# Low parts of the second FFN's down weights: from a subtraction on VectorE to a negated cast on ScalarE and an accumulating DMA

## The chip, the cores and the metric

The kernel runs on one core of a Trainium2 chip. A core has five engines with a queue of instructions each: TensorE (PE, matrix products), VectorE (DVE), ScalarE (ACT), GpSimd (POOL) and SyncE (SP, which issues the transfers), and 16 DMA engines between the memory and the on-chip buffer. An engine works through its queue in order and waits on semaphores. The metric is the device time of one execution in microseconds.

## The reference

Two decoder layers over 512 tokens of width 1024, each `x += gate1 * Mixer(adaLN(x))` and `x += gate2 * ConvFFN(adaLN(x))`. Layer 0 mixes by attention, layer 1 by a state-space layer and a gated delta rule. The change touches only the FFN of layer 1:

```python
def conv_ffn(h, w_up, conv_w, w_down):
    up = causal_dwconv(h @ w_up, conv_w)
    a, b = jnp.split(up, 2, axis=-1)
    return (jax.nn.silu(a) * b) @ w_down
```

`w_up` is 1024 x 5632, `w_down` 2816 x 1024, all in float32.

## The kernel before

Activations lie transposed, 128 channels on the partitions and 512 tokens in a row. Every large product is made of three: each float32 factor is split into a high part, rounded to the type fp32r, and a low part, which is the factor minus its high part; the product is high x high, high x low and low x high, added up in one bank of PSUM (`mm3`, L374 to L376). So every weight needs two tiles, `whi` and `wlo`.

A weight is got ready by `prep` (L343 to L361): SP loads it into a staging tile `st` (L356, two of them in turn), ACT casts it to `whi` (L359), and DVE writes `wlo` as `st` minus `whi` (L360). There are five tiles `whi` and five `wlo` in turn; a cast waits until PE has done with the weight that held the tile before. `weight` asks for a weight one or two places ahead of its use, in the order of `weight_order`.

The second FFN (`ffn` with l = 1) goes over 22 channel blocks j of the up projection. The first four are plain products. From j = 4 a pair of up weights is made into seven smaller products of 256 columns (`prep_pair`, L315 to L341, and `seven`, L594 to L627). `prep_pair` uses the same staging tiles for its loads of an even block (L321 and L322), and the same tiles `whi` and `wlo`; DVE adds in the staging tiles (L335 to L339) and subtracts (L328), ACT casts (L327). In `seven`, ACT copies intermediate products from PSUM (L610, tiles p1, p7 and p16), and PE goes on with the same bank after that; DVE makes `ub` and `ua` (L620 to L624). `finish` does the convolution, the SiLU (L657) and the split of the result into `gh` and `gl`.

The down projection is cut by GROUPS into four groups of 6, 6, 5 and 5 blocks, with 8 weights each: 32 down weights (`dn`, 1), 16 of 128 x 768 and 16 of 128 x 640. The weights of a group come one or two per block among the up products of the next group, a product of 18 or 15 matmuls of 512 columns each (L374 to L376 with `gh` and `gl`); those of the last group come at the end (`out_gemm`). A DVE instruction then adds the result to x (L479), and SP stores x (L1612).

The order of the instructions on each engine is set when the program is built, by a scheduler that goes by priorities and dependences. Nothing is issued to POOL in this FFN before the change.

Of the kernel before, what the change touches and what calls it, by code (L numbers as in the profile page):

```python
# [8 lines left out]
F32 = mybir.dt.float32  # L9
F32R = mybir.dt.float32r  # L10
I32 = mybir.dt.int32
AF = mybir.ActivationFunctionType
ALU = mybir.AluOpType
# [176 lines left out]
def down_after(l, j):  # L190
# [3 lines left out]
    if q == 0:  # L194
        return []
    if not SPREAD[l]:
        return [(q - 1, m) for m in range(8 if j == g[q] else 0)]
# [43 lines left out]
SPLIT_AT = (18, 18, 18, 18)  # L241
FAST = ((), tuple(range(4, 22)))
SPREAD = (False, True)
REC_K = (2, 3, 4, 5, 0, 1, 6, 7)


class Kernel:
# [95 lines left out]
    def prep(self, pool=None, stage=None):  # L343
        key = self.order[self.next]
        self.next += 1
        if key[0] == "sp":
            self.ready[key] = self.prep_pair(*key[1:])
            return
        src, n = self.source(key)
        nc = self.nc  # L350
        wp = pool or self.wp
        if stage:
            st = stage[0].tile([P, 1024], F32, name="ast", tag=stage[1], bufs=stage[2])[:, :n]
        else:
            st = wp.tile([P, 1024], F32, name="st", tag="st", bufs=1 if pool else 2)[:, :n]
        nc.sync.dma_start(st, src)  # L356
        hi = wp.tile([P, 1024], F32R, name="whi", tag="whi", bufs=1 if pool else 5)[:, :n]
        lo = wp.tile([P, 1024], F32R, name="wlo", tag="wlo", bufs=1 if pool else 5)[:, :n]
        nc.scalar.copy(hi, st)  # L359
        nc.vector.tensor_tensor(lo, st, hi.bitcast(F32), ALU.subtract)  # L360
        self.ready[key] = (hi, lo)  # L361

    def weight(self, key):
# [730 lines left out]
    def recurrent(self):  # L1094
# [450 lines left out]
        rhs = self.pairs(self.hB)  # L1545
        for n, a in zip(REC_K, SPLIT_AT):
            self.tc.cur_priority = at[a]
            self.split(Y[n], *rhs[n], half=n < 2)
        self.tc.cur_priority = end
        for n in REC_K[len(SPLIT_AT):]:  # L1550
            self.split(Y[n], *rhs[n], half=n < 2)
# [6 lines left out]
        self.keep, self.keep_pool = {}, self.open("fg1", "right")  # L1558
        self.out_gemm([("ro", m) for m in range(8)], rhs, lambda m: self.gate(1, 0, m), 1, 1, hC, REC_K, ("acc", "acc", "t", "x", "s", "s", "o", "o"))
        self.close("hB")  # L1560
# [90 lines left out]
```

## Time and profile before

| what | value |
|---|---|
| median of 3 runs | 1306.91 us (1306.52 to 1307.76) |
| the profiled execution | 1305.8 us |
| its span | 1304.0 us |
| PE busy in the span | 1280.3 us (98%) |
| DVE busy | 1011.4 us (78%) |
| ACT busy | 638.8 us (49%) |
| POOL busy | 3.6 us |
| clock of TensorE | full speed in every slice |
| DMA, mean | 139 GB/s |

The span is what the profile covers; the profiled execution took 1.8 us more than that, and its time is 1.1 us below the median. The share of an engine is a mean over stages with different limits. A matmul's end is modelled and matmuls overlap, so the distance from one start to the next tells PE's pace better than the durations. A row of the chain or the timeline that names a releaser in brackets says how long the engine was idle before that instruction and what ended the wait.

### The profile page before, as it was taken

How to read it: one execution, taken by the hardware profiler on the slowest of the kernel's cores; microseconds unless marked ns; L12 is line 12 of the kernel's file. 1: busy time of each engine (PE TensorE's matmuls, PEld its weight loads, DVE VectorE, ACT ScalarE, POOL GpSimd, SP SyncE). 2: the span in 40 equal slices, each digit the busy share in tenths (PEclk: the TensorE clock that was granted, in tenths of full speed). 3: DMA queues.
4: the chain of work that ended last, by engine and by line, in shares of the span. 5: the costliest groups of instructions: out<-in, count | busy, mean ns of one | idle time of the engine just before them, and what ended most of it. 6: DMA issues, size and time to landing. Idle time of an engine off the chain costs nothing.

```text
span 1304.0 us, 22696 instructions
## 1 busy us (share of the span) xinstructions
PE 1280.3 (98%) x8814; PEld 1085.3 (83%) x8814; DVE 1011.4 (78%) x2227; ACT 638.8 (49%) x1246; POOL 3.6 (0%) x11
## 2 busy tenths in 40 slices
PE   8989999999999999999999999999999999999998
PEld 5976776798886888888898888887898998999998
DVE  6886856579996589477578786775699988988883
ACT  4446566435441333233357545654475655555550
POOL 0000000000000000000000000000000000000000
PEclk9999999999999999999999999999999999999999
DMA  9763511425655477454343531221322322333222
GB/s 364 272 226 118 186 59 48 164 105 192 213 163 169 159 263 241 154 185 157 106 176 127 140 111 44 102 60 34 130 98 98 105 102 102 102 102 99 96 85 102
DMA packets 83131, 181.13 MB, mean 139 GB/s; under 512 B 28560, under 2 KB 36176, under 8 KB 83024
## 3 DMA queue, kind: packets, MB, share of 16 engines
q1 hardware_dynamic: 83024, 179.69, 40.8%
q8 instruction: 69, 1.13, 0.3%
q14 instruction: 38, 0.31, 0.1%
HBM read 165.55 MB, written 14.11 MB: 138 GB/s over the span
## 4 chain that ended last, share of the span: by engine, by line
PE 86%; DVE 6%; DMA 3%; ACT 2%; issue 2%; SPq 0%; DVEq 0%; ACTq 0%
PE acc L374 10%; PE acc L375 10%; PE acc L376 10%; PE s L375 5%; PE s L376 5%; PE s L374 5%; PE o L375 4%; PE o L376 4%; PE o L374 4%; PE s L606 3%; PE s L776 3%; PE o L606 3%; PE acc L606 3%; PE o L805 2%; DMA ast<-ada 1%
## 5 line engine op out<-in xcount | busy, mean ns | idle before, releaser
L359 ACT CAST whi<-st 128x1024 fp32r<-128x1024 f32 (+3 forms) x168 | 165.2, 987 | 213.5 <-PE acc L375 69.6
L360 DVE TENSOR_TENSOR wlo<-st,whi 128x1024 fp32r<-128x1024 f32 (+3 forms) x168 | 191.5, 1142 | 50.8 <-ACT whi L359 49.3
L374 PE MATMUL acc<-hh,whi 128*128 128x512 f32 (+1 forms) x392 | 141.1, 365 | 0.5 <-ACT hh L530 0.5
L375 PE MATMUL acc<-hl,whi 128*128 128x512 f32 (+1 forms) x392 | 140.9, 363 | 0.2 <-DVE hl L394 0.2
L376 PE MATMUL acc<-hh,wlo 128*128 128x512 f32 (+1 forms) x392 | 140.8, 362 | 0.0
L445 DVE CUSTOM_DVE_ANT_0 adaj<-ast,cond 128x1024 bf16<-128x1024 f32 x86 | 105.0, 1221 | 11.9 <-DMA ast<-ada 11.5
L375 PE MATMUL acc<-wlo,hh 128*128 128x256 f32 x320 | 92.9, 291 | 0.0
L374 PE MATMUL acc<-whi,hh 128*128 128x256 f32 x320 | 92.1, 288 | 0.6 <-ACT hh L530 0.6
L376 PE MATMUL acc<-whi,hl 128*128 128x256 f32 x320 | 91.3, 287 | 0.9 <-DVE hl L531 0.9
L375 PE MATMUL s<-hl,whi 128*128 128x512 f32 (+2 forms) x256 | 86.8, 339 | 0.0
L376 PE MATMUL s<-hh,wlo 128*128 128x512 f32 (+2 forms) x256 | 86.6, 338 | 0.0
L374 PE MATMUL s<-hh,whi 128*128 128x512 f32 (+2 forms) x256 | 86.4, 338 | 0.0
L375 PEld LDWEIGHTS acc<-hl,whi 128*128 128x128 f32 x392 | 73.3, 188 | 12.7 <-DVE hl L394 1.2
L374 PEld LDWEIGHTS acc<-hh,whi 128*128 128x128 f32 x392 | 73.1, 188 | 12.2 <-ACT hh L530 0.8
L376 PEld LDWEIGHTS acc<-hh,wlo 128*128 128x128 f32 x392 | 73.4, 188 | 11.2 <-issue 0.7
L327 ACT CAST whi<-st 128x1024 fp32r<-128x1024 f32 x54 | 56.4, 1049 | 32.5 <-DVE st L339 9.3
L328 DVE TENSOR_TENSOR wlo<-st,whi 128x1024 fp32r<-128x1024 f32 x54 | 65.9, 1222 | 4.4 <-ACT whi L327 4.4
L374 PE MATMUL o<-hh,whi 128*128 128x512 f32 (+1 forms) x192 | 69.0, 359 | 0.0
L375 PE MATMUL o<-hl,whi 128*128 128x512 f32 (+1 forms) x192 | 68.9, 359 | 0.0
L376 PE MATMUL o<-hh,wlo 128*128 128x512 f32 (+1 forms) x192 | 68.8, 358 | 0.0
L374 PEld LDWEIGHTS acc<-whi,hh 128*128 128x128 f32 x320 | 60.3, 188 | 4.9 <-issue 3.2
L375 PEld LDWEIGHTS acc<-wlo,hh 128*128 128x128 f32 x320 | 60.3, 188 | 3.9 <-issue 3.7
(910 smaller groups left out, 3498.7 us busy)
## 6 DMA issues: line engine op xcount, KB each, us to landing
ast<-ada SPq DMA_DIRECT2D x92, 512.0 KB
st<-up SPq DMA_DIRECT2D x88, 512.0 KB
st<-ri SPq DMA_DIRECT2D x20, 512.0 KB
st<-wq SPq DMA_DIRECT2D x17, 512.0 KB
st<-dn SPq DMA_DIRECT2D x16, 448.0 KB
st<-dn SPq DMA_DIRECT2D x16, 384.0 KB
st<-dn SPq DMA_DIRECT2D x16, 320.0 KB
st<-wo SPq DMA_DIRECT2D x8, 512.0 KB
```

What stands on the lines that cost most here:

```text
L327: nc.scalar.copy(hi, src)
L328: nc.vector.tensor_tensor(lo, src, hi.bitcast(F32), ALU.subtract)
L359: nc.scalar.copy(hi, st)
L360: nc.vector.tensor_tensor(lo, st, hi.bitcast(F32), ALU.subtract)
L374: mm(out, lh, rh, start=start, stop=False)
L375: mm(out, lh, rl, start=False, stop=False)
L376: mm(out, ll, rh, start=False, stop=stop)
L445: self.nc.vector.tensor_tensor_reduce(junk, st, self.cond, 1.0, 0.0, op0=ALU.mult, op1=ALU.add, accum_out=self.md[l][:, i:i + 1])
L606: nc.tensor.matmul(acc, x[:, s], y, start=start and k == n == 0, stop=k == 3 and n == 2, skip_group_check=not start)
L776: nc.tensor.matmul(sb, qT[pr, i * P:(i + 1) * P], kT[pr, j0 * P:(i + 1) * P], start=True, stop=True)
L805: nc.tensor.matmul(ob[64 * par:64 * par + 64, i * P:(i + 1) * P], V[:, j0 + j, vc:vc + 64], pts[:, par, j * P:(j + 1) * P], start=j == 0, ...
```

## The change

For the weights whose key begins with ("dn", 1), the low part is made in another way. ACT casts the staged weight to `whi` as before. Then ACT also writes minus `whi` into `wlo`, and POOL issues a transfer that reads the weight from memory a second time and adds it to what stands in `wlo`. DVE has no part in it. All other weights are made as before.

```diff
+DMA_LOW = (("dn", 1),)
...
         nc.scalar.copy(hi, st)
-        nc.vector.tensor_tensor(lo, st, hi.bitcast(F32), ALU.subtract)
+        if key[:2] in DMA_LOW:
+
+            nc.scalar.activation(lo, hi.bitcast(F32), AF.Copy, scale=-1.0)
+            nc.gpsimd.dma_start(lo, src, accum_op=ALU.add)
+        else:
+            nc.vector.tensor_tensor(lo, st, hi.bitcast(F32), ALU.subtract)
```

Lines behind L360 move down by six. So L374, L375 and L376 become L380, L381 and L382, L606 becomes L612 and L610 becomes L616; the new cast is L363 and the new transfer L364. L327 and L328 become L328 and L329 by one, and L359 becomes L360.

The scheduler also sets another order. First, ACT at the first down weight. Before (whi_11062 is the high part of that weight; whi_11070 belongs to the next pair of up weights):

```order
L610 COPY p7_11121<-x_11091 128x256
L359 CAST whi_11062<-st_11060 128x768
L327 CAST whi_11070<-st_11066 128x1024
L610 COPY p16_11135<-t_11090 128x256
L657 ACTIVATE ta_11046<-ta_11046 128x512
```

ACT at the same place, changed:

```order
L616 COPY p7_11122<-x_11092 128x256
L360 CAST whi_11062<-st_11060 128x768
L328 CAST whi_11071<-st_11067 128x1024
L363 ACTIVATE wlo_11063<-whi_11062 128x768
L616 COPY p16_11136<-t_11091 128x256
L663 ACTIVATE ta_11046<-ta_11046 128x512
```

The new cast stands behind the cast of the up weight and ahead of the copy p16.

Second, PE at the same weight (the product goes into the bank acc; rows of products that are alike are left out). Before, with no other product between the high and the low part:

```order
L606 MATMUL t_11090<-b30l_10367,whi_10938 128x256
L606 MATMUL t_11090<-b30h_10366,wlo_10939 128x256
L374 MATMUL acc_11203<-gh_10604,whi_11062 128x512
L375 MATMUL acc_11203<-gl_10605,whi_11062 128x512
L376 MATMUL acc_11203<-gh_10604,wlo_11063 128x512
```

PE at the same place, changed:

```order
L380 MATMUL acc_11204<-gh_10604,whi_11062 128x512
L381 MATMUL acc_11204<-gl_10605,whi_11062 128x512
L612 MATMUL s_11255<-hh0_10080,whi_11071 128x256
L612 MATMUL t_11091<-b00h_10324,whi_10938 128x256
...
L612 MATMUL t_11091<-b30h_10366,wlo_10939 128x256
L612 MATMUL s_11255<-hl0_10081,whi_11071 128x256
...
L612 MATMUL s_11255<-hh3_10086,wlo_11072 128x256
L612 MATMUL o_11257<-hh4_10088,whi_11071 128x256
L382 MATMUL acc_11204<-gh_10604,wlo_11063 128x512
```

Between the first high and the first low part now stand the 12 products into t, which stood ahead of the weight before, and 13 more into s and o.

Third, ACT at the third down weight (whi_11369 before, whi_11371 changed). Before:

```order
L610 COPY p1_11415<-t_11398 128x256
L327 CAST whi_11249<-st_11229 128x1024
L657 ACTIVATE ta_11352<-ta_11352 128x512
L610 COPY p7_11429<-x_11399 128x256
L359 CAST whi_11369<-st_11367 128x768
```

ACT at the same place, changed:

```order
L328 CAST whi_11251<-st_11231 128x1024
L360 CAST whi_11371<-st_11369 128x768
L616 COPY p1_11419<-t_11402 128x256
L663 ACTIVATE ta_11354<-ta_11354 128x512
L363 ACTIVATE wlo_11372<-whi_11371 128x768
L616 COPY p7_11433<-x_11403 128x256
```

The high cast of the down weight has moved ahead of the copy p1. Behind the first steps the order of PE differs at two more places by a few rows, and is the same from there on.

## Rows read from the trace of the kernel before

**Rows 1.** Windows: busy time of each engine, clock, DMA share, GB/s.

```profile
core 0: us, PE busy (x) PEld busy (x) DVE busy (x) ACT busy (x) POOL busy (x), PEclk, DMA share, GB/s
1026.00:1304.00 278.00, 271.97 (x1879) 251.03 (x1877) 228.07 (x334) 138.36 (x217) 0.00 (x0) 1.00 0.29 101
```

**Rows 2.** Timeline of PE: start us, us, instruction, idle before and releaser.

```profile
1085.27 0.28 PE L606 MATMUL acc<-hh,wlo 128*128 128x256 f32 x1
1087.16 0.39 PE L606 MATMUL acc<-b01h,vhi 128*128 128x256 f32 x1 [1.61 <-ACT p L610]
...
1204.14 0.28 PE L606 MATMUL acc<-hh,wlo 128*128 128x256 f32 x1
1204.97 0.38 PE L606 MATMUL x<-hh,whi 128*128 128x256 f32 x1 [0.56 <-DVE ub L622]
...
1234.47 0.28 PE L606 MATMUL s<-hh,wlo 128*128 128x256 f32 x1
1235.14 0.38 PE L606 MATMUL acc<-hh,whi 128*128 128x256 f32 x1 [0.40 <-DVE ub L622]
```

**Rows 3.** Chain that ended last, 1066 to 1237: start us, us, what.

```profile
1068.21 0.96 DVE wlo L360
...
1069.19 4.53 DMA st<-up
...
1080.31 4.20 DMA st<-dn
...
1084.54 0.84 ACT whi L359
...
1196.37 3.99 DMA st<-up
...
1226.50 1.37 PE acc L606 x12
...
1228.26 3.91 DMA st<-up
```

**Rows 4.** Groups by form, 1020 to 1304: count, busy us, mean ns, idle before.

```profile
L360 DVE TENSOR_TENSOR wlo<-st,whi 128x768 fp32r<-128x768 f32 x16 | 15.3, 954 | 1.7 <-ACT whi L359 1.7
L359 ACT CAST whi<-st 128x768 fp32r<-128x768 f32 x16 | 13.4, 838 | 10.5 <-DMA st<-dn 4.4 <-PE s L375 3.2 <-PE o L375 2.1
L360 DVE TENSOR_TENSOR wlo<-st,whi 128x640 fp32r<-128x640 f32 x16 | 13.1, 822 | 1.4 <-ACT whi L359 1.4
L359 ACT CAST whi<-st 128x640 fp32r<-128x640 f32 x16 | 11.6, 729 | 15.9 <-DMA st<-dn 6.8 <-PE acc L375 5.4 <-PE acc L606 2.3
```

**Rows 5.** Timeline of ACT at five down weights.

```profile
1024.16 0.84 ACT L359 CAST whi<-st 128x768 fp32r<-128x768 f32 x1 [0.34 <-DMA st<-dn]
1024.90 1.05 ACT L327 CAST whi<-st 128x1024 fp32r<-128x1024 f32 x1
...
1051.85 0.84 ACT L359 CAST whi<-st 128x768 fp32r<-128x768 f32 x1 [0.18 <-DMA st<-dn]
...
1066.72 0.83 ACT L359 CAST whi<-st 128x768 fp32r<-128x768 f32 x1
...
1124.41 0.84 ACT L359 CAST whi<-st 128x768 fp32r<-128x768 f32 x1
...
1284.74 0.73 ACT L359 CAST whi<-st 128x640 fp32r<-128x640 f32 x1 [4.13 <-DMA st<-dn]
```

**Rows 6.** Timeline of SP's queue, 1048 to 1050.

```profile
1048.99 0.33 SPq L356 DMA_DIRECT2D st<-dn  x1
```

**Rows 7.** Timeline of PE: first reads of three down weights' low parts.

```profile
1028.71 0.39 PE L376 MATMUL acc<-gh,wlo 128*128 128x512 f32 x1
...
1138.46 0.39 PE L376 MATMUL x<-gh,wlo 128*128 128x512 f32 x1
...
1292.10 0.28 PE L376 MATMUL acc<-gh,wlo 128*128 128x256 f32 x1
```

**Rows 8.** Waits of ACT, 1026 to 1304: us in total, times, longest.

```profile
ACT p L610 <- PE s L606: 8.4, 9, 1.8
```

## The prediction

> **What bounds the kernel now.** I read the views in this order: the busy time of the stretch that the change touches, the few places where TensorE (PE) idles there, the chain that leads to each of them, then the subtraction that goes, then how early each low part is needed.
>
> The stretch runs from 1026 us, where the first subtraction for a down weight of the second FFN stands, to the end. In its 278 us PE is busy for 271.97, VectorE (DVE) for 228.07, ScalarE (ACT) for 138.36, GpSimd (POOL) not at all, and the DMA engines have a share of 0.29 [rows 1]. A busy PE is not always PE at its pace, so I take the pace from starts: twelve products of 256 columns took 1.37 us, 0.114 each [rows 3]. PE falls out of that pace at three places behind 1026. From the start of one matmul to that of the next it took 1.89 us at 1085.27, 0.83 at 1204.14 and 0.67 at 1234.47 where 0.11 is the rule [rows 2]. That is 1.78 + 0.72 + 0.56 = 3.1 us, and it is nearly all that PE can get back: the stretch is bound by PE, and DVE is the engine that is late at these places.
>
> The chain shows why, with the largest one. The subtraction L360 of a down weight starts at 1068.21 and frees a staging tile; the load of an up weight follows (4.53 us), then a run of DVE work, then a load of a down weight (4.20 us), its cast on ACT at 1084.54, and behind that cast the copy of a product for which PE waits at 1087.16 [rows 2, 3]. The gaps at 1204.97 and 1235.14 are waits for DVE's ub [rows 2]; the chain to each holds a load of an up weight into a staging tile, issued at 1196.37 and 1228.26 [rows 3].
>
> **The change, part by part.** *Removed:* 32 subtractions on DVE, 16 of 0.954 us and 16 of 0.822 [rows 4], 28.4 us of DVE's 228. DVE is not on PE's path except at the three places, so the worth is at most their 3.1 us. I take all of it, because two things come together. DVE has some 0.9 us less to do per down weight. And the staging tile is now free when the high part's cast ends: the cast that belongs to 1068.21 ran from 1066.72 for 0.83 us [rows 5], so the tile is free at 1067.6 where the load waited until 1069.19 [rows 3]; 1.6 us earlier, almost the 1.78 of the gap behind it. Term: -3.1 us. What cover this needs: ACT must not be late in its turn.
>
> *Added on ACT:* 32 times minus the high part, ACT from fp32r tile to tile. I price them as the casts of the same tile sizes, 16 of 0.838 and 16 of 0.729 us [rows 4], 25.1 us. ACT is busy for half of the stretch [rows 1], and it mostly waits for PE when it copies products (L610): 9 waits for the s banks alone are 8.4 us [rows 8]. The new casts fall into such waits. I take 0. Queued behind a new cast on ACT are the copies of products (p), the SiLU and the next high part. Where the cover is gone it costs up to 1.7 us once: at the third down weight the order puts its high cast, which waited for a landing until 1051.85 [rows 5], ahead of the copy p1; PE has one other product of 1.4 us to do in that time. With PE already late by the next term, it is hidden.
>
> *Added on POOL and the DMA queue:* 32 accumulating transfers, 16 of 384 KB and 16 of 320 KB, 11.5 MB more than the 28 MB (101 GB/s in 278 us) that the stretch moves now. The share of 0.29 [rows 1] grows to 0.41, or to 0.53 if the old low part is counted as read too; bandwidth is not the limit. POOL has nothing else queued there [rows 1]. SP's queue keeps the 32 loads of the staging tile, so every down weight is now read twice from memory.
>
> *The path from weight to matmul.* Before: high cast, subtraction (0.95 us), matmul. Now: high cast, low cast, transfer, matmul. No transfer issued by POOL and none that accumulates is in the trace, so its time T from the end of the low cast to the release of PE is bounded. Below: a plain load of the same 384 KB, issued at 1048.99 and waited for by ACT until 1051.85, 2.9 us [rows 5, 6]. Above: twice the slowest load of that size, 4.20 us [rows 3], 8.4. A gain is excluded, since nothing gets ready sooner by it. I take twice the quick load, 5.7 us: two operands of that size come in, and the queue is lightly used, so the quick load is the nearer row.
>
> The transfer is late where PE comes soonest after the high cast. That is the first down weight: its cast starts at 1024.16, another cast of 1.05 us at 1024.90 stands behind it, and PE read the low part at 1028.71 [rows 5, 7]. In the new order the low cast stands behind that second cast, so it ends at 1024.90 + 1.05 + 0.84 = 1026.8; and PE has 13 more products of 256 columns ahead of the first low part, 13 x 0.114 = 1.5 us, so it comes at 1030.2. With T = 5.7 the tile is there at 1032.5: PE waits for 2.3 us. The bounds of T give 0 and 5.0.
>
> For later weights the same sum finds no wait. A usual one: high cast from 1124.41 for 0.84 us, low part read at 1138.46 [rows 5, 7], 13.2 us apart. The tightest late one is the last weight of all: cast from 1284.74 for 0.73 us, read at 1292.10 [rows 5, 7], 6.6 us apart; its load too goes out earlier, by about the 1.6 us above, so low cast and transfer have 8.2 us where 0.73 + 5.7 = 6.4 are needed.
>
> *By the skill's price:* the Trainium skill (DMA: Bandwidth & Descriptors, section "Anatomy of one DMA — SWDGE (gpsimd) path") fits transfers issued by GpSimd as 2.0 us plus the bytes at 436 GB/s, for 384 KB an estimate of 2.9 us. No run here shows such a transfer, and the fit is for plain ones; by it the first weight's wait is 0 and the sum -3.1, so 1303.8.
>
> *Sum.* The profiled execution took 1305.8 us (span 1304.0), 1.1 below the median of 1306.91. 1305.8 - 3.1 + 0 + 2.3 = 1305.0 in its own terms, 1306.1 in terms of the median. With T at its bounds: 1303.8 and 1308.8. So I forecast no difference that can be told: a measurement of this kernel tells about 0.2%, 2.6 us, apart.
>
> **The rivals.** *Faster.* The transfer is as quick as a plain load (T near 2.9), PE never waits for a low part, and all three gaps close: 1306.9 - 3.1 = 1303.8. For it: nothing else uses POOL, and the DMA engines are idle for 0.71 of the stretch [rows 1]. Against it: two operands instead of one, a longer hand-over (ACT, POOL, queue, PE), and there is no more than 3.1 us to have, so any wait above 0.5 us ends it.
>
> *Slower: the accumulating transfer itself is slow.* Place: PE's first low part, and then every weight that PE reads within T of its cast. It decides from a first wait of 3.1 + 2.6 = 5.7 us, thus T = 9.1 us. For T = 12: 1026.8 + 12 - 1030.2 = 8.6 us at the first weight. The last weight would be late by 12 + 0.73 - 8.2 = 4.5 us, but PE itself then comes 8.6 - 3.1 = 5.5 later, so it adds none; 1306.9 - 3.1 + 8.6 = 1312.4. Above T = 13 the usual distance of 13.2 us [rows 5, 7] doesn't cover it either, and each further us adds at many weights. For it: the operation was never seen here, and reads its destination. Against it: engines that are idle for most of the time.
>
> *Slower: DVE holds back GpSimd.* If POOL can prepare transfers only while DVE is idle, 0.18 of the time [rows 1], a microsecond of preparation becomes 1 / 0.18 = 5.5 us. T = 5.7 + 4.5 = 10.2, the first wait 6.8 and the time 1306.9 - 3.1 + 6.8 = 1310.6. The rule is in the Trainium skill (SBUF — State Buffer, section "Who interferes with whom"): GpSimd and DVE share a port pair, and an instruction of DVE in a 2-port mode shuts GpSimd out. The page also says that tensor_tensor has no such mode, and that is most of what DVE runs here; no run here shows it, as POOL is idle.
>
> *The change does nothing:* that PE is bound and both terms are small is the forecast itself.
>
> **How the numbers follow.** Forecast 0.45 (1304.3 to 1309.5, its own range, with T between 3.9 and 9.1), faster 0.24, slow transfer 0.25, DVE against GpSimd 0.06. So faster 0.24, same 0.45, slower 0.31. The range goes down to 1303.3 (the faster case, with half a us for what the pace itself regains) and up to 1315 (T near 13); above it lies the rest of the slow transfer, some 0.12, and below it some 0.05.
>
> **What would show it.** Right: PE's one new wait stands at the first read of a low part near 1030 and is 1 to 4 us long, released by a DMA; the gaps at 1085, 1204 and 1235 are gone or under 0.3 us; DVE's busy time falls by 28 us, ACT's grows by about 25; low tiles land 4 to 8 us after POOL's issue. Wrong: PE waits for a low part at many weights (then T is above 9), ACT's copies of products are late behind the new casts (then PE's waits name ACT), or the three gaps stay (then DVE was not what they hung on). It would be wrong in the other direction if PE never waits.

## The result

The changed kernel is slower: 1317.41 us, median of 5 runs (1315.17 to 1325.87), beside 1307.76 for the kernel before (1306.52 to 1309.59). The ratio is 1.0078, with a 95% interval of 1.0055 to 1.0102, so about 10 us. The prediction was 1306.1, with a range that ended at 1315.0.

| run | what is changed | ratio to the kernel before | 95% interval |
|---|---|---|---|
| the changed kernel | all 32 low parts by transfer | 1.0078 | 1.0055 to 1.0102 |
| r1_cast_behind | one order edge on ACT | 1.0073 | 1.0051 to 1.0094 |
| r2_both | that edge, first weight on DVE | 1.0067 | 1.0040 to 1.0094 |
| r3_no_transfer | ACT writes, DVE adds | 1.0003 | 0.9989 to 1.0017 |
| r4_first_on_vector | first weight on DVE | 1.0053 | 1.0032 to 1.0073 |
| r5_transfers_only | kernel before plus transfers that nobody reads | 1.0179 | 1.0157 to 1.0201 |
| r6_cast_ahead | kernel before, a cast ahead of a copy | 1.0003 | 0.9991 to 1.0016 |
| r7_loads_in_turn | other order of loads on SP | 1.0056 | 1.0035 to 1.0078 |
| r8_half_transfer | half by transfer, half by DVE | 1.0105 | 1.0088 to 1.0122 |
| r9_changed_without_transfers | the transfers left out | 0.9968 | 0.9947 to 0.9990 |
| r10_plain_transfers | plain transfers, not adding | 1.0015 | 0.9993 to 1.0038 |
| r11_every_other | every other weight, the rest on DVE | 1.0006 | 0.9985 to 1.0026 |
| r12_half_bytes | half the columns of each transfer | 1.0024 | 1.0006 to 1.0043 |
| r13_half_number | every other transfer | 1.0013 | 0.9995 to 1.0030 |
| r14_three_weights | the new way for three weights | 0.9976 | 0.9966 to 0.9986 |

Each ratio goes against runs of the kernel before that were taken with it (their medians lie between 1307.8 and 1311.0 us), so the ratios are to be compared, and not the times. They are the ratios on record; the ratio of the two medians lies up to 0.0014 from them (r10), so a difference of 0.001 between two rows tells nothing. r9, r10, r12 and r13 leave out a part of the low parts' arithmetic and serve for timing alone.

### The profile page after: what moved, and what is told of

It reads as the page before. It is cut to its first block, busy times and chain, and to the rows that moved or that the text cites. A ratio compares the mean times of both kernels' runs of the same rounds, so it can differ in the third digit from the quotient of the medians.

```text
span 1315.6 us, 22783 instructions
## 1 busy us (share of the span) xinstructions
PE 1285.0 (98%) x8814; PEld 1089.4 (83%) x8814; DVE 988.7 (75%) x2195; ACT 659.2 (50%) x1278; POOL 31.1 (2%) x43
## 5 line engine op out<-in xcount | busy, mean ns | idle before, releaser
L360 ACT CAST whi<-st 128x1024 fp32r<-128x1024 f32 (+3 forms) x168 | 165.0, 985 | 215.9 <-PE acc L381 65.6
L366 DVE TENSOR_TENSOR wlo<-st,whi 128x1024 fp32r<-128x1024 f32 (+1 forms) x136 | 162.8, 1199 | 49.0 <-ACT whi L360 47.5
L380 PE MATMUL acc<-hh,whi 128*128 128x512 f32 (+1 forms) x392 | 141.1, 365 | 1.4 <-ACT hh L536 1.3
L381 PE MATMUL acc<-hl,whi 128*128 128x512 f32 (+1 forms) x392 | 140.8, 362 | 0.2 <-DVE hl L400 0.2
L382 PE MATMUL acc<-hh,wlo 128*128 128x512 f32 (+1 forms) x392 | 140.7, 362 | 0.0
L451 DVE CUSTOM_DVE_ANT_0 adaj<-ast,cond 128x1024 bf16<-128x1024 f32 x86 | 104.7, 1218 | 11.2 <-DMA ast<-ada 10.9
L381 PE MATMUL acc<-wlo,hh 128*128 128x256 f32 x320 | 93.3, 292 | 0.0
L380 PE MATMUL acc<-whi,hh 128*128 128x256 f32 x320 | 92.4, 289 | 0.6 <-ACT hh L536 0.6
L382 PE MATMUL acc<-whi,hl 128*128 128x256 f32 x320 | 91.6, 288 | 0.9 <-DVE hl L537 0.9
L381 PE MATMUL s<-hl,whi 128*128 128x512 f32 (+2 forms) x256 | 86.7, 339 | 0.0
L380 PE MATMUL s<-hh,whi 128*128 128x512 f32 (+2 forms) x256 | 86.4, 337 | 0.0
L382 PE MATMUL s<-hh,wlo 128*128 128x512 f32 (+2 forms) x256 | 86.4, 337 | 0.0
L380 PEld LDWEIGHTS acc<-hh,whi 128*128 128x128 f32 x392 | 73.1, 188 | 13.1 <-ACT hh L536 1.6
L381 PEld LDWEIGHTS acc<-hl,whi 128*128 128x128 f32 x392 | 73.3, 188 | 12.6 <-DVE hl L400 1.2
L382 PEld LDWEIGHTS acc<-hh,wlo 128*128 128x128 f32 x392 | 73.3, 188 | 11.2 <-issue 0.7
L329 DVE TENSOR_TENSOR wlo<-st,whi 128x1024 fp32r<-128x1024 f32 x54 | 65.7, 1218 | 5.1 <-ACT whi L328 4.9
L328 ACT CAST whi<-st 128x1024 fp32r<-128x1024 f32 x54 | 56.3, 1046 | 25.6 <-PE o L612 5.6
L380 PE MATMUL o<-hh,whi 128*128 128x512 f32 (+1 forms) x192 | 69.0, 359 | 0.0
L382 PE MATMUL o<-hh,wlo 128*128 128x512 f32 (+1 forms) x192 | 69.0, 359 | 0.0
L381 PE MATMUL o<-hl,whi 128*128 128x512 f32 (+1 forms) x192 | 68.9, 359 | 0.0
L380 PEld LDWEIGHTS acc<-whi,hh 128*128 128x128 f32 x320 | 60.4, 189 | 4.9 <-issue 3.2
L381 PEld LDWEIGHTS acc<-wlo,hh 128*128 128x128 f32 x320 | 60.3, 188 | 3.9 <-issue 3.7
```

The lines of the kernel that those rows point to most:

```text
L328: nc.scalar.copy(hi, src)
L329: nc.vector.tensor_tensor(lo, src, hi.bitcast(F32), ALU.subtract)
L380: mm(out, lh, rh, start=start, stop=False)
L381: mm(out, lh, rl, start=False, stop=False)
L382: mm(out, ll, rh, start=False, stop=stop)
L451: self.nc.vector.tensor_tensor_reduce(junk, st, self.cond, 1.0, 0.0, op0=ALU.mult, op1=ALU.add, accum_out=self.md[l][:, i:i + 1])
```

## The profile after

First the stretch of [rows 1]. The row below has the same columns: the stretch, busy us and counts of PE, PEld, DVE, ACT and POOL, the granted clock, the DMA share and GB/s.

```profile
1026.00:1304.00 278.00, 269.94 (x1832) 248.99 (x1831) 204.27 (x300) 160.11 (x251) 27.80 (x32) 0.99 0.53 139
```

DVE lost 24 us of work, ACT took on 22, POOL does nothing but issue the 32 transfers, and the DMA share went from 0.29 to 0.53. Here the old gaps of [rows 2] are not to be found; PE waits elsewhere. These are the four waits above 1 us in the timeline of PE (start, us, instruction, idle before and releaser), each with the matmul before it:

```profile
1030.89 0.28 PE L612 MATMUL o<-hh,whi 128*128 128x256 f32 x1
1033.48 0.50 PE L382 MATMUL acc<-gh,wlo 128*128 128x512 f32 x1 [2.32 <-DMA wlo<-dn]
...
1104.41 0.28 PE L612 MATMUL o<-b31h,vlo 128*128 128x256 f32 x1
1106.01 0.38 PE L612 MATMUL s<-b00h,whi 128*128 128x256 f32 x1 [1.33 <-ACT p L616]
...
1137.95 0.28 PE L612 MATMUL o<-b31h,vlo 128*128 128x256 f32 x1
1140.16 0.45 PE L612 MATMUL o<-b00h,whi 128*128 128x256 f32 x1 [1.92 <-ACT p L616]
...
1173.40 0.28 PE L612 MATMUL t<-b31h,vlo 128*128 128x256 f32 x1
1176.12 0.39 PE L612 MATMUL o<-b00h,whi 128*128 128x256 f32 x1 [2.44 <-ACT p L616]
```

From start to start, less the 0.11 us that a product of 256 columns takes, they cost 2.48, 1.49, 2.10 and 2.61 us, 8.7 in all. The first is the late low part that was forecast. The other three were not: PE waits for ACT's copy `p16` (L616). Why the copy is late stands in ACT's own timeline at the first of them:

```profile
1100.84 0.35 ACT L616 COPY p<-s 128x256 f32<-128x256 f32 x1
1101.10 0.62 ACT L399 CAST gh<-tb 128x512 fp32r<-128x512 f32 x1
1101.89 0.37 ACT L616 COPY p<-o 128x256 f32<-128x256 f32 x1 [0.18 <-PE o L612]
1105.07 0.62 ACT L328 CAST vhi<-st 128x512 fp32r<-128x512 f32 x1 [2.81 <-DMA st<-up]
1105.60 0.37 ACT L616 COPY p<-s 128x256 f32<-128x256 f32 x1
```

The two copies at 1100.84 and 1101.89 are `p1` and `p7`. The third, `p16`, stands behind the cast `vhi`, and that cast belongs to the next pair: it waits 2.81 us for an up load to land, with the copy that PE needs queued behind it. In the chain of waits (start, us, what) the load is the long piece:

```profile
1098.84 0.84 ACT whi L360
...
1099.69 5.35 DMA st<-up
...
1105.07 0.03 ACT vhi L328
```

In [rows 3] loads of up weights take 3.91 to 4.53 us; here 5.35, and at the two other waits 5.80 and 6.32 (issued at 1133.39 and 1168.84).

There is a second loss behind two of the waits. The rows below are of the granted clock (the last number but two), in windows of 1 us after the wait that ends at 1033.48:

```profile
1033.00:1034.00 1.00, 0.52 (x2) 0.47 (x3) 1.00 (x2) 0.21 (x1) 0.00 (x0) 1.00 0.00 0
1034.00:1035.00 1.00, 1.00 (x5) 0.77 (x5) 1.00 (x2) 0.00 (x0) 0.00 (x0) 0.76 0.20 37
1035.00:1036.00 1.00, 1.00 (x7) 1.00 (x6) 0.17 (x1) 0.00 (x0) 0.00 (x0) 0.50 0.89 299
```

The clock is at its lower level, 1.2 GHz, from within 1034 to within 1037. The wider windows around the two falls give what it took: 0.95 over 1030 to 1035, 0.71 over 1035 to 1040 and 0.83 over 1140 to 1150, so 5 x 0.05 + 5 x 0.29 + 10 x 0.17 = 3.4 us, 1.7 for each fall. Behind the waits of 1106 and 1176 the clock stayed at 1.00.

## The experiments

### Theory and rivals

At first I held that ACT's new order did it (theory A: `vhi` ahead of `p16`), with these rivals: the transfers make the loads late (B), the first late low part and its clock (C), ACT's 25 us of casts as such (D).

**The cast behind the copy.** The edge is written at the trace of a pair: its `vhi` cast may not be issued ahead of the last `p16` traced.

```diff
-        f["22"], = halves(b[:, T:], self.fp, "v", 2)
...
+            with self.tc.issue_after(self.p16.ins):
+                f["22"], = halves(b[:, T:], self.fp, "v", 2)
...
```

> The changed kernel with one order edge more: the cast of a pair's second load (vhi) may not be issued on ScalarE ahead of the copy p16 of the pair before. In the changed kernel's profile TensorE waited 1.49, 2.10 and 2.61 us for that copy, which stood behind a vhi cast that waited 2.81, 3.37 and 3.88 us for its load, and the granted clock fell once after one of these waits (about 1.7 us). One of the three places in which the cast stands ahead of the copy is left by this edge. Theory A (ScalarE's order makes the loss): 1317.4 - 6.2 - 1.7 = 1309.5 us, up to 1312 if the place that is left still waits. Rival B (the accumulating transfers slow the loads, and TensorE then waits for the loads themselves): 1317, with the same waits under another name. Rival C (only the first late low part and its clock matter): 1317. Rival D (25 us more work on ScalarE): 1317.

Measured 1.0073: nothing won. The waits for `p16` went, and others came in their place, of 3.77, 1.68 and 1.84 us from start to start, for DVE's `ub`; the first low part was late by 3.29 us in that profile, the slowest execution of the six. DVE's timeline at the first of them shows the same queue on the other engine:

```profile
1111.88 0.69 DVE L329 TENSOR_TENSOR vlo<-st,vhi 128x512 fp32r<-128x512 f32 x1 [5.82 <-ACT vhi L328]
1112.48 0.42 DVE L632 SCALAR_TENSOR_TENSOR ub<-o,p 128x256 f32<-128x256 f32 x1
...
1114.02 0.42 DVE L634 SCALAR_TENSOR_TENSOR ub<-s,p 128x256 f32<-128x256 f32 x1
```

`vlo` of the next pair stands ahead of `ub` of this one, and waits through `vhi` for the same load. So ACT's order decides where PE feels the late load, but not whether it does. Theory A fell here in its simple form.

**The first down weight on DVE again**, alone (r4) and with the edge (r2). The edit takes out one weight, the first of the first column group, in r2 too (the expectation speaks of one in each group):

```diff
-        if key[:2] in DMA_LOW:
+        if key[:2] in DMA_LOW and key[2:] != (0, 0):
```

> The changed kernel, the low part of the first down weight alone (first row block of the first column group) made by VectorE as before; ScalarE's order is else that of the changed kernel, cast ahead of copy at most pairs. Theory A and C: the first wait (2.5 us) and the halved clock behind it (1.7 us) go, the waits for the copy p16 stay: 1317.4 - 4.2 = 1313.2 us. If the first wait were the whole of the loss: 1307. If a wait costs no clock: 1314.9.

> The same order edge, and the low part of the first down weight of each column group, first row block, is made by VectorE as before, so that no accumulating transfer stands in front of the stage's first down matmuls. Theory A with C: 1309.5 less the first wait of 2.5 us and the clock after it of 1.7 us: 1305.3 us. Rival B: about 1313 (only the first wait goes). Rival D: 1313.

Measured 1.0053 and 1.0067. The wait at 1030 is gone in both, though in r2 another low part is late by 2.02 us, at 1062. Both intervals overlap that of the changed kernel: a gain of 4.2 us would be 0.3%, and the ratios leave 0.1 to 0.25%. In r4's profile the three waits for `p16` grew, to 1.98, 2.54 and 3.23 us (6.2 us in the changed kernel, 7.75 here). The longest of them:

```profile
1172.98 0.28 PE L612 MATMUL t<-b31h,vlo 128*128 128x256 f32 x1
1176.32 0.38 PE L612 MATMUL o<-b00h,whi 128*128 128x256 f32 x1 [3.06 <-ACT p L616]
```

PE comes to the same places sooner, and the loads take longer: 5.70, 6.25 and 7.08 us in the chain, where the changed kernel has 5.35, 5.80 and 6.32. Rival C is out as the whole of the loss. What the first wait is worth alone these intervals don't tell: they hold both nothing and the 4.2 us.

**No transfer, DVE adds.**

```diff
-            nc.gpsimd.dma_start(lo, src, accum_op=ALU.add)
+            nc.vector.tensor_tensor(lo, lo.bitcast(F32), st, ALU.add)
```

> No accumulating transfer at all: ScalarE still writes minus the high part (25 us more on ScalarE), and VectorE adds the staged weight to it. ScalarE's order comes out as that of the run with both edits, with the copy p16 ahead of the casts nearly everywhere. Theory A: no loss from ScalarE's work as such, 1306 to 1309 us. Rival B (transfers): 1306 to 1309 as well, but with the loads of the up weights back at 3.9 to 4.5 us where the run with both edits shows over 5.3. Rival D (ScalarE's load): 1313 or more.

Measured 1.0003. ACT has its extra 25 us here and nothing is lost, so rival D is out. Waits of 1.87, 0.73 and 1.10 us from start to start stand near the places of the old gaps, so nothing is won there either. The order was not that of the run with both edits, as I had written: SP's order came out as in the kernel before, since DVE reads the staging tile again. The run doesn't tell A from B therefore.

**The order without transfers**, in the kernel before:

```diff
...
-        p16 = keep(Z, "p16")
+        with self.tc.issue_after(self.vcast.ins):
+            p16 = keep(Z, "p16")
```

> The kernel before, without any transfer, with the copy p16 held behind the vhi cast of the next pair at each pair, as ScalarE has it in the changed kernel at the three places of the waits. Theory A (order alone): in the kernel before the load that this cast waits for is issued at 1100.18 us and loads take 3.9 to 4.5 us, so the copy of 1100.81 us would come at about 1104.3, some 3.5 us late, of which the 12 matmuls between cover 1.4: 2.1 us at each of four or five places and the clock behind them: 1307.8 + 8 to 12 = 1316 to 1320 us. Theory B1 (load of the DMA engines): at most the slack, 1308 to 1310 us. B2 (both are needed): between, 1309 to 1313 us, with waits under 1.5 us each.

Measured 1.0003. This is weak evidence: the cast traced last was often that of the pair in work, so the edge put a cast ahead of a copy at three pairs more than before, and none of them is one of the three with the waits. The better test of the same question is r9, below.

**Transfers alone**, in the kernel before. They add the weight to a scratch tensor in memory; a copy of one column on POOL holds each back until the high part is there.

```diff
         nc.vector.tensor_tensor(lo, st, hi.bitcast(F32), ALU.subtract)
+        if key[:2] == ("dn", 1):
...
+            g = nc.gpsimd.tensor_copy(self.tiny, hi[:, :1].bitcast(F32))
+            with self.tc.issue_after(g.ins):
+                nc.gpsimd.dma_start(self.w1.rearrange("p a t -> p (a t)")[:, :n], src, accum_op=ALU.add)
```

> The kernel before, unchanged in the order of TensorE, VectorE, ScalarE and SyncE, with 32 accumulating transfers added whose result nobody reads: once a second-FFN down weight's high part is there, GpSimd issues a transfer that adds the same weight to a scratch tensor in DRAM (not to SBUF, where there is no room for a scratch). Theory B1 (the DMA engines' load alone makes the loads late and TensorE wait): 1307.8 + 6 to 9 us = 1314 to 1317 us. Theory B2 (late loads cost only where work that waits for them stands ahead of the pair's own copies and combinations on ScalarE and VectorE, which in this order it mostly doesn't): 1307.8 to 1311 us, with loads at over 5 us all the same. Theory A (order alone): 1307.8 us, unchanged.

Measured 1.0179, worse than any of the expectations. Orders on PE, ACT, DVE and SP are those of the kernel before, and PE now waits for ACT's copies `p` and DVE's `ub` (2.28, 2.50, 2.61 and 2.14 us from start to start at 1096, 1149, 1218 and 1255), with up loads of 4.42 to 6.91 us in the chain. From the matmul that starts at 1027.81 to the last one at 1323.82 the stage takes 296.0 us; the same two starts lie 279.6 apart in the kernel before. That is 16.4 us for transfers that nobody reads, in the order of the kernel before. They add into memory and not into the on-chip buffer, so this isn't the price in the changed kernel. Two things are not the transfers' effect on loads: the last transfers still run when PE is done, since they go into one scratch and wait for each other (the last issue is below), and one cast of a high part waited 1.2 us for POOL's copy.

```profile
1327.29 0.81 POOL L365 DMA_DIRECT2D w<-dn  x1 [4.45 <-DMA w<-dn]
```

**The loads in turn.** SP's order in the changed kernel is, for two pairs, first load of the later pair, first of the earlier, second of the later, second of the earlier, because the earlier one shares its staging tiles with the down weights and gets them last. Here both loads of a pair go ahead of those of the next.

```diff
...
+            with self.tc.issue_after(self.bload.ins):
+                nc.sync.dma_start(a, self.I["up"][l, j])
+                self.bload = nc.sync.dma_start(b, self.I["up"][l, NJ + j])
...
```

> The changed kernel with another order of loads on SyncE: both loads of the pair that is used first (its staging tiles are shared with the down weights and come free last) ahead of both loads of the pair behind it, in place of a2, a1, b2, b1. ScalarE's order keeps the vhi cast ahead of p16 at the three places. The load that the cast waits for is then issued behind no other up load, with the accumulating transfers alone beside it. B1 and B2: it lands 1 to 2 us sooner, the three waits of 1.49, 2.10 and 2.61 us shrink to under 1 us each and the clock behind them stays: 1317.4 - 4 to 6 = 1311.4 to 1313.4 us. Theory A without a share of the queue: unchanged, 1317 us. If the loads of the pair behind then come late in turn: 1317 or more, with TensorE waiting for a whi cast of that pair.

Measured 1.0056. The three waits together shrank from 6.2 to 4.2 us (1.85, 1.28, 1.09), with loads of 5.56, 4.99 and 4.80, and two waits for a low part of 0.8 us each came up at other weights. In the three waits the order of the up loads has a share; the ratio doesn't tell it, as its interval overlaps that of the changed kernel. A load with only the first one of its own pair ahead of it, issued 4.0 us before, still took 4.8 us or more.

**Half by transfer, half by DVE.**

```diff
+            c = n // 2
+            nc.scalar.activation(lo[:, :c], hi[:, :c].bitcast(F32), AF.Copy, scale=-1.0)
+            nc.gpsimd.dma_start(lo[:, :c], src[:, :c], accum_op=ALU.add)
+            nc.vector.tensor_tensor(lo[:, c:], st[:, c:], hi[:, c:].bitcast(F32), ALU.subtract)
```

> The changed kernel with half of each low part (the first half of its columns) made by ScalarE and the transfer, the other half by VectorE's subtraction as before: 32 transfers of half the bytes. B (bytes on the DMA engines): half the loss, 1307.8 + 4 to 6 = 1312 to 1314 us, the share of the DMA engines about 0.41. If the number of transfers rather than their bytes costs: 1317. If the release of the staging tile (VectorE reads it again here, so SyncE's order is that of the kernel before) is what counts: 1308 to 1309.

Measured 1.0105, no gain over whole transfers (the two intervals overlap), where every expectation but one had a gain. Since DVE reads the staging tile here, this mixes two causes; the next five runs price the transfers by themselves.

### The transfers taken out, and what they cost

**All transfers left out**, nothing in their place:

```diff
-            nc.gpsimd.dma_start(lo, src, accum_op=ALU.add)
```

> The changed kernel with the 32 accumulating transfers left out and nothing in their place, so the low parts hold minus the high part and the addition of the weights is left out. ScalarE still writes all low parts, VectorE still has no pass, the staging tile still comes free after ScalarE's cast alone, SyncE's order is that of the changed kernel, and at the three places of the waits the vhi cast still stands ahead of p16. Theory B (the transfers beside the loads cost it all): no late first low part, loads at 3 to 4.5 us, waits for p16 under 0.5 us: 1307.8 less the old gaps of 3.1 us = 1304.7 us, between 1303 and 1308. Theory A (order on ScalarE, with or without transfers): 1317.4 - 2.5 - 1.7 = 1313 us. Rival D (25 us of ScalarE): 1313 to 1317.

Measured 0.9968, within what B had. This is the run that decides. SP's order is that of the changed kernel, ACT's too but for a few rows, and the cast still stands ahead of the copy at the three places. The same place in ACT's timeline, and then the load that the cast waits for, in SP's:

```profile
1097.84 0.37 ACT L615 COPY p<-o 128x256 f32<-128x256 f32 x1
1098.93 0.62 ACT L328 CAST vhi<-st 128x512 fp32r<-128x512 f32 x1 [0.73 <-DMA st<-up]
1099.46 0.37 ACT L615 COPY p<-s 128x256 f32<-128x256 f32 x1
```

```profile
1095.74 0.33 SPq L323 DMA_DIRECT2D st<-up  x1
```

Issued at 1095.74 and cast at 1098.93, the load took 3.19 us where it takes 5.38 with the transfers (1099.69 to 1105.07). The wait of `vhi` is 0.73 in place of 2.81, and PE has none above 0.35 us in the whole stretch behind 1026. So theory A is out as a cause on its own, and rival B holds: the order costs only where the load is late, and the load is late because of the transfers. How full the DMA engines are while the four loads run is in the following rows, the changed kernel first, then without transfers (a window of 10.8 us that begins as the first of the four is issued, and the part of it that ends as the fourth has landed):

```profile
1094.30:1105.10 10.80, 10.39 (x72) 9.44 (x70) 6.43 (x10) 6.05 (x12) 1.73 (x2) 1.00 0.90 247
```

```profile
1090.50:1101.30 10.80, 10.80 (x79) 10.06 (x78) 8.07 (x13) 7.50 (x14) 0.00 (x0) 1.00 0.55 196
1090.50:1098.95 8.45, 8.45 (x59) 7.71 (x58) 6.39 (x9) 6.00 (x12) 0.00 (x0) 1.00 0.69 248
```

A share of 0.53 over the stage was 0.90 in the 10.8 us in which the load that matters was under way, and 0.69 without transfers. At the two other places it is 0.84 and 0.89, and 0.67 and 0.68 without.

The account closes to within what one profiled execution of each can tell. From the matmul ahead of the small wait near 1021 to the last matmul, in the changed kernel and without transfers:

```profile
1021.67 0.28 PE L612 MATMUL x<-b00l,whi 128*128 128x256 f32 x1
...
1310.30 0.28 PE L382 MATMUL acc<-gh,wlo 128*128 128x256 f32 x1
```

```profile
1021.62 0.28 PE L611 MATMUL x<-b00l,whi 128*128 128x256 f32 x1
...
1297.78 0.28 PE L381 MATMUL acc<-gh,wlo 128*128 128x256 f32 x1
```

288.6 against 276.2 us, 12.5 us for the transfers, of which the four waits are 8.7 and the clock 3.4. Against the kernel before (279.6) the change without its transfers gains 3.4, and the gaps of [rows 2] were 3.1. That these agree to 0.3 us is in part luck: PE's own pace differs by more. In the trace of the kernel before, twelve products of 256 columns take 1.41 us in one place and 1.36 in another, at a granted clock of 1.00 in both, and the slower places aren't the same in every trace (in the ten microseconds from 1150 on a product took 0.115 us before and 0.118 without transfers):

```profile
1096.53 1.41 PE s L606 x12
...
1153.28 1.36 PE s L606 x12
```

By the ratios, 1.0078 / 0.9968 = 1.011, the transfers cost about 14 us and the rest of the change gains about 4.

**Plain transfers** of the same bytes in the same order:

```diff
-            nc.gpsimd.dma_start(lo, src, accum_op=ALU.add)
+            nc.gpsimd.dma_start(lo, src)
```

> The changed kernel in its own order throughout, with each of the 32 transfers a plain one of the same bytes on the same GpSimd queue instead of an accumulating one: the low parts then hold the whole weights, and minus the high part is left out of them. If it is the adding that makes the transfers costly (they took 23.9% of the DMA engines' time for 11.54 MB where the loads took 29.0% for 26.87 MB): landing in about 4 us in place of 5.7, a share of 0.13 in place of 0.24, loads at 4 to 5 us, 1308 to 1313 us. If any transfer of GpSimd's queue beside the loads costs the same: 1317 us, with loads at 5.3 to 6.3 us.

Measured 1.0015, about half of the price: 0.43 of it by the ratios, 0.56 by the stage (283.2 us, where it is 276.2 without transfers and 288.6 with adding ones). The DMA queues of the stretch 1026 to 1304 (packets, MB, share of the 16 engines' time), in the changed kernel and here:

```profile
q1 hardware_dynamic: 9072, 26.87, 29.0%
q0 software_dynamic: 4608, 11.54, 23.9%
```

```profile
q1 hardware_dynamic: 9307, 27.32, 29.2%
q0 software_dynamic: 4608, 11.54, 14.4%
```

For the same bytes an adding transfer holds the engines for 0.239 x 278 / 32 = 2.08 us (as if all 16 did it), a plain one for 1.25. The landings, from the two rows on the tile `wlo`:

```profile
DMA to landing us min/median/max: 4.2/5.7/7.9
```

```profile
DMA to landing us min/median/max: 3.3/4.1/6.2
```

The loads at the three places take 4.73, 4.45 and 4.45 us, between those without and those with adding, and so do the waits for `p16`: 1.02, 0.74 and 0.73. The first low part is still late by 2.16 us.

**Half the bytes, half the number.** In r12 each transfer has the first half of its columns only; in r13 every other transfer is left out; in r11 the weights without transfer are made by DVE.

The three edits, in this order:

```diff
-            nc.gpsimd.dma_start(lo, src, accum_op=ALU.add)
+            nc.gpsimd.dma_start(lo[:, :n // 2], src[:, :n // 2], accum_op=ALU.add)
```

```diff
+            if key[3] % 2:
                 nc.gpsimd.dma_start(lo, src, accum_op=ALU.add)
```

```diff
-        if key[:2] in DMA_LOW:
+        if key[:2] in DMA_LOW and key[3] % 2 == 1:
```

> The changed kernel with each of the 32 accumulating transfers cut to the first half of its columns and nothing in place of the rest: half of each low part is left without the addition of the weights. The orders of ScalarE, VectorE and SyncE are those of the run without transfers but for the transfers themselves. That run came out at 0.9968 of the kernel before, the changed kernel at 1.0078. If the price of the transfers goes with their bytes: half way, a ratio of 1.002 (1310 to 1312 us). If it goes with their number, as the run with half transfers beside VectorE's half pass (1.0105) lets one think: 1.006 to 1.008. If halves fit between the loads: 0.997 to 0.999.

> The changed kernel with the accumulating transfers of every other down weight alone (second, fourth and so on of each column group), whole, and nothing in place of the others: half of the low parts are left without the addition. VectorE makes no pass in their place, so against the run with every other weight on VectorE (1.0006) this shows what VectorE's passes and the later release of the staging tile add there. If the price goes with number or bytes: 1.002 less the first wait, 0.999 to 1.002. If one transfer per group of four loads makes the last load as late as two do: 1.004 to 1.006. If only two do: 0.997 to 0.999.

> The changed kernel with transfers for every other down weight alone (the second, fourth and so on of each column group), the others' low parts by VectorE as before: 16 transfers of whole size, and the first down weight is not among them. If the loss goes with the number of transfers: half of the transfers' cost and no first wait, 1307.8 + 3 to 5 = 1311 to 1313 us. If one transfer beside a group of four loads is enough to make the last load late: 1315 to 1317. If only pairs of transfers at the same group do: 1308 to 1309 us.

Measured 1.0024, 1.0013 and 1.0006. Between 0.9968 and 1.0078 half way is 1.0023, so both halves are near it: in the changed kernel's order the price goes with what the transfers hold of the DMA engines (0.135 and 0.133 of the stretch here, 0.239 whole), and whether by bytes or by number makes no difference that these intervals can tell. r11 and r13 agree too, so DVE's passes for the other half of the weights cost nothing there. The slowness of r8 (1.0105, against 1.0024 for r12 with the same transfers) then comes with DVE's half pass on every weight. r8 and r5 have in common that DVE reads the staging tile and that SP's order is that of the kernel before, and both lose more than a run without that: r8 more than r12, r5 more than the changed kernel. r8's profile shows the staging tile of the late load read by DVE until 1104.82 and the load issued at 1104.85, behind ACT's cast of 1103.38; that it is this later release that makes the difference is argued from there, no run isolates it.

**Three weights.** The gain without transfers should hang on three staging tiles, as the prediction's chain had it. So the new way for the three weights that lead to the old gaps, and the old way for the other 29:

```diff
-DMA_LOW = (("dn", 1),)
+DMA_LOW = (("dn", 1, 0, 4), ("dn", 1, 2, 0), ("dn", 1, 2, 3))
-        if key[:2] in DMA_LOW:
+        if key in DMA_LOW:
```

> The kernel before with the new way for three of the 32 down weights alone, and VectorE's subtraction for the others: the three whose subtraction, in the chain of the kernel before, frees the staging tile of the load that ends in one of the old gaps (the subtractions at 1068.21, 1195.47 and 1227.38 us). If each of the gaps hangs on its staging tile and a lone transfer costs little (the sixteen of the run with half the number cost 1.0013 against 0.9968, some 0.4 us each): 1307.8 - 3.1 + 1 = 1305 to 1306 us, a ratio of 0.998 to 0.999. If the gaps hang on VectorE's load in all, or one lone transfer delays the load that its early release gained: no change, 1.000. If the new casts hold up copies there: 1.001 to 1.002.

Measured 0.9976 (0.9966 to 0.9986): faster than both kernels, and somewhat more than expected. The row of the stretch, and the one wait of PE above 0.3 us that is left between 1060 and 1300:

```profile
1026.00:1304.00 278.00, 273.74 (x1887) 252.05 (x1885) 227.68 (x333) 141.29 (x221) 2.71 (x3) 1.00 0.34 105
```

```profile
1168.57 0.39 PE L612 MATMUL o<-hh,whi 128*128 128x256 f32 x1 [0.40 <-DVE ub L628]
```

DVE is as busy as in [rows 1] (227.68 against 228.07), and yet the three gaps of [rows 2] are gone: it was the three weights with their staging tiles, not DVE's work in all. At the first of them the load is issued at 1068.81, as the cast of 1067.95 ends, where before it waited 1.6 us more for the subtraction. The subtraction itself is gone from DVE's queue there too; no run has the one without the other. The gain rests on the ratio: in the one profiled execution the stage is 278.5 us, 1.2 shorter than before and not 3.1, and PE's own pace can differ by that much from trace to trace.

## Why the prediction failed, step by step

- **What bounds the stage, and the gain of 3.1 us: right.** The gaps are gone in the changed kernel, without transfers the stage is 3.4 us shorter (ratio 0.9968), and r14 has a gain of that size (0.9976) with DVE as busy as before. The chain of [rows 3] named the staging tiles, and doing three weights alone the new way bears it out.
- **ACT's 25 us at nothing: right as work, wrong as a place in a queue.** The new casts took 25.2 us by their durations, and r3, which carries them, is at 1.0003. The one place that I had named, the third down weight, cost nothing. But the scheduler's new order put a cast that waits for a load ahead of a copy that PE waits for, at three places that I had not looked at. I had listed what stands behind the new casts, and not compared what each new neighbour waits for. The sign was in the trace of the kernel before, among the waits of ACT of which [rows 8] shows one; here with the same wait in the changed kernel (in total, times, longest):

```profile
ACT vhi L327 <- DMA st<-up: 9.1, 6, 2.7
```

```profile
ACT vhi L328 <- DMA st<-up: 13.1, 6, 3.9
```

- **The transfer's own time, 5.7 us: right, with some luck.** Median 5.7, from 4.2 to 7.9, and the first wait of PE cost 2.48 us, from 1030.89 on, where 2.3 us from 1030.2 on was forecast. No other weight's low part is late. But 5.7 was twice a quick load for a lightly used queue, and the landings were measured among loads that filled the engines. The Trainium skill (DMA: Bandwidth & Descriptors, "Anatomy of one DMA — SWDGE (gpsimd) path") gives an estimate of 2.9 us by its fit for a plain transfer of 384 KB; the plain ones of r10 of that size, among the loads, took 4.0 at the median, so trace and page differ; the measurement decides.
- **"Bandwidth is not the limit": this step failed.** The share of 0.53 that I gave as the upper end came true to the digit. From a mean of 0.53 over 278 us I concluded that nothing is delayed, and gave the transfers no price beside their own landing. But the four loads of two pairs go out within 6 us, one transfer is issued among them and another just behind them, and there the engines were at 0.90. The loads took 5.35 to 6.32 us where [rows 3] has 3.91 to 4.53, ACT waited for them in order, and PE waited for ACT. That is 6.2 us of waits. With the transfers left out and the order kept, the late loads, the waits and the loss are gone (r9, 0.9968). That the staging tile's earlier release, which I counted as pure gain, sends these loads out in one bunch with the transfers adds to the loss isn't shown: r5 and r8, without that release, lost more.
- **No price for the clock.** A wait was priced at its length. Two of the four were followed by half the clock, 3.4 us more. The two missed terms are 6.2 + 3.4 = 9.6 of the 11.3 us between forecast and result. In the profiled executions the difference is 12.4 us (1317.41 against the 1305.0 of the sum): these 9.6, 0.2 at the first wait, 1.0 because the stretch begins later (1021.67 against 1020.65), and 1.6 because the end of the span comes 5.3 us behind the last matmul's start and not 3.7; what makes the last two isn't shown. The clock's part isn't the same in every execution: over the five of the changed kernel the mean clock went from 0.992 to 0.999 and the time from 1325.87 to 1315.17, so even the best of them is 7.4 us above the kernel before.
- **The rivals.** The slower rival had the right sign but for the wrong reason: it asked for a transfer of over 9.1 us. (The range ended at 1315 for T near 13, where the sum itself gives 1306.9 - 3.1 + 9.6 = 1313.4; the result lies above both.) The rival that DVE holds back GpSimd is not borne out: the issue on POOL took 862 ns at the least and at the median, 1128 at most, with DVE busy for 0.73 of the stretch. The rule of the Trainium skill (SBUF — State Buffer, "Who interferes with whom") is not refuted by that, since it gives tensor_tensor no 2-port mode, and that is most of what DVE ran.
- **What would show it wrong** was written down rightly: "ACT's copies of products are late behind the new casts (then PE's waits name ACT)". The name came true, with another cast in front than the new ones.

## What to carry to other kernels

A mean share of the DMA engines can hide a late load that others wait for (0.53 in the mean, 0.90 around the load here): look at the share in the few microseconds in which that load runs, and at what stands behind its consumer on each in-order engine. Here an edit that frees a buffer early and pays for it in transfers was worth it only where that buffer gated something: three weights of 32 had the gain (0.9976), and the other 29 turned it into a loss. When a wait is removed and another engine's name takes its place, as long or longer (6.2 and then 7.3 us in r1), the late thing is further up: leave out the suspected resource itself, and keep the order.

## What the runs showed of the hardware

An accumulating transfer from memory into the on-chip buffer held the DMA engines for 2.08 us on the mean of 384 and 320 KB, a plain one from the same queue for 1.25 (23.9% against 14.4% of the stretch), and its issue took POOL 862 ns against 527. An up load of 512 KB took 5.38 us beside the adding transfers and 3.19 without (r9), from issue to the start of its cast. The clock of TensorE fell to 1.2 GHz behind waits of 2.48 and 2.10 us and stayed there for some 3 us while PE had work again, yet not behind waits of 1.49 and 2.61 us in the same run.
